# Experts in pairs: chunks of two experts alternate, and each down projection follows its chunk by one

## The chip, the cores and the metric

The kernel runs on one core of a Trainium2 chip. TensorE (PE) multiplies, PEld is its weight load, VectorE (DVE) and ScalarE (ACT) work on vectors, GpSimd (POOL) does little here, and SyncE (SP) issues the weight transfers. The metric is the device time of one execution in microseconds (us), the median of several runs.

## The reference

A backbone of two layers over 256 tokens of 1024 channels, batch 1, in float32. What matters here is the feed-forward part of the second layer, a SwiGLU of 8 experts with 3584 hidden channels, of which each token uses the two with the highest router logits:

```python
def moe_swiglu(h, w_router, b_router, w1, w3, w2):
    logits = (h @ w_router).astype(jnp.float32) + b_router.astype(jnp.float32)
    top_val, top_idx = lax.top_k(logits, TOP_K)
    top_w = jax.nn.softmax(top_val, axis=-1)
    gate = jnp.einsum('blk,blke->ble', top_w, jax.nn.one_hot(top_idx, N_EXPERTS, dtype=jnp.float32)).astype(h.dtype)
    out = jnp.zeros_like(h)
    for e in range(N_EXPERTS):
        out = out + gate[..., e:e + 1] * swiglu(h, w1[e], w3[e], w2[e])
    return out
```

With the given inputs the router sends 67, 37, 16, 137, 46, 15, 130 and 64 tokens to experts 0 to 7, 512 in all.

## The kernel before

Everything up to the router (both mixers, the dense feed-forward, the Fourier layer) is the same in both kernels. The experts' stage begins at about 579 us of the profiled execution.

**Positions.** Expert 0 comes first, since its weights can be loaded before the router is done. The others are sorted by their counts on the chip (L1345 to L1363), and `ORDER` (L29) says which rank stands at which position: 0, then ranks 6, 1, 7, 3, 2, 5, 4 (rank 1 has most tokens). Here the positions hold 67, 16, 137, 15, 64, 130, 37 and 46 tokens. The counts go into registers of PE, ACT and DVE (L1324, L1534), and the SP queue takes the experts' indices from registers (L1530).

**Units.** An expert's gathered tokens are handled in units of 64, at most three (`NU`, L1370); what lies past 192 tokens is left to a late pass (L1621 to L1642). A unit with 32 tokens or fewer in it runs as a half. Which units run is decided by nested `If`s on the counts, with an arm for the full and one for the half form: `base_unit` (L1417) for the first unit, `extra_units` (L1403) for the others, to the depth that `most` (L1391) bounds by the rank: the k-th largest count is at most 512 / k. So position 4 has code for three units and position 6 for two, whatever the counts. Position 0's first unit stands in no `If`.

**Chunks.** The 3584 hidden channels go in seven chunks of 512 (`NS`, L1368). For a chunk, `up_proj` (L1426) multiplies the unit's tokens with both up matrices in eight steps k, into one PSUM bank; SiLU on ACT (L1446) and the product on DVE (L1447) make the activations `a`. In the next chunk, at step k = 3, `flip` (L1449) transposes them, and DVE copies them to `aT` (L1454). `down_proj` (L1456) multiplies `aT` with the down matrix and adds into the expert's own PSUM bank over the seven chunks; after the last, `collect` (L1474) copies the sums to SBUF.

**Order.** The loop over positions (L1526) runs the up projection of expert e and the down projection of expert e - 1, chunk by chunk: up of the first unit in one `If`, up of the other units in a nest of `If`s, then the down projections in two more (for the first chunk the down projections come before the other units' up projections). All seven `aT` of the old expert are kept until then. After the eighth expert a ninth turn (`e == NE`) does seven chunks of down projections alone. Smaller work is put between the steps of the first unit's up projection (`work`, L1556): gate weights and scatter of the expert before the old one (L1557 to L1560, third unit L1608), one-hot and gather for the next expert (L1561 to L1565), the gate of the layer (L1567).

**Transfers.** All weights come through `load` (L60) on the SP queue, 1 MB each, into a ring of 18 slots. A chunk takes four for the up projection (`load_up`, L1513) and two for the down projection (`load_down`, L1518). A slot is free when the last arm that reads it has ended. The loads of the first expert are issued from 508 us on.

Of the kernel before, what the change touches and what calls it, by code (L numbers as in the profile page):

```python
# [11 lines left out]
OP = mybir.AluOpType  # L12
AX = mybir.AxisListType
# [15 lines left out]
ORDER = (0, 6, 1, 7, 3, 2, 5, 4)  # L29
# [5 lines left out]
def backbone(ctx, tc, x, c, cx, c_ctx, w_ada, b_ada, norm_g, w_in, short_w, short_b,  # L35
# [291 lines left out]
    # implicit filters and their spectra; even positions come first, then odd ones, and the second  # L327
    # half of the frequencies mirrors the first
# [142 lines left out]
    # the convolution branch, as a list of steps issued between the attention heads  # L471
# [247 lines left out]
    # the gate of a branch scales the columns of its last weights  # L719
# [6 lines left out]
    # the clock of the tensor engine falls while it idles  # L726
# [12 lines left out]
    # the same by column halves: the first half becomes the bias of the root  # L739
# [14 lines left out]
    # sums over the partitions: columns of two vectors at a time, or a row on all partitions  # L754
# [31 lines left out]
    with ExitStack() as es:  # L786
# [11 lines left out]
        # modulation vectors of what follows, a step of 256 rows of their weights at a time  # L798
# [70 lines left out]
        # the first one as its rows become ready  # L869
# [75 lines left out]
        for n in range(NU2):  # L945
# [44 lines left out]
            # the last ones wait, for the end  # L990
# [170 lines left out]
        # router weights for the raw rows  # L1161
# [76 lines left out]
    hg0 = [T(mp, [P, ND, P], f"hg0{b}") for b in range(2)]  # L1238
# [21 lines left out]
    with ExitStack() as es:  # L1260
        rp = mkpool("route", es=es)
        xT = T(rp, [P, 2, 2, 4, P], "xT")
        # logits from the raw rows, four parts of the channels side by side; scale and shift follow
# [35 lines left out]
        # places in the order of the logits, the first of equal ones before the others  # L1299
# [21 lines left out]
        nc.vector.tensor_copy(cnt[:, 2, 1:2], ps[0:1, 0:1])  # L1321
        gather(spread, P, hg0[0], [acc[1][0], acc[1][1]])
# [22 lines left out]
        # the experts after the first are taken in an order that follows their counts  # L1345
# [16 lines left out]
        nc.vector.reduce_max(key[0:1, 0:1], sorted_[0:1, 4, :], axis=AX.X)  # L1362
# [6 lines left out]
    NU = 3  # L1369
# [8 lines left out]
    ysb0 = T(up, [P, 2, 512], "ysb0")  # L1378
    ysb1 = T(up, [P, 512], "ysb1")
# [8 lines left out]
    LATE = 64 * NU  # L1388
    side = lambda u, j: j ^ (u & 1)
    # the k-th largest of the sorted counts is at most S * 2 / k  # L1390
    most = lambda e: S if e == 0 else min(S, 2 * S // ORDER[e])  # L1391

    class Expert:
        def __init__(self, e):
            self.e = e

        def rows(self, u):
            return hg1 if u == 2 else hg0[self.e % 2][:, :, 64 * u:64 * u + 64]

        def low(self, u, i):  # L1400
            return 64 * ((self.e * NS + i) % 2 if u == 0 else u % 2)

    def extra_units(E_, fn):  # L1403
        def level(u):
            with tc.If(counts[E_.e] > 64 * u):  # L1405
# [7 lines left out]
                if u < NU - 1 and most(E_.e) > 64 * (u + 1):  # L1413
                    level(u + 1)
        level(1)

    def base_unit(E_, fn):  # L1417
        if E_.e == 0:
            fn(False)
            return  # L1420
        with tc.If(counts[E_.e] > 32) as arm:
            fn(False)
        with arm.Else():
            fn(True)
# [298 lines left out]
```

## Time and profile before

| | us |
|---|---|
| three runs | 1638.01, 1643.89, 1647.61 |
| median | 1643.89 |
| profiled execution: its own time | not listed beside the runs; its span stands for it |
| profiled execution: span, first to last instruction | 1633.9 |
| of it PE busy | 1485.8 (91%) |
| DVE, ACT busy | 616.3, 319.0 |
| moved by DMA in all | 470 MB, mean 288 GB/s |

The profile puts each instruction under the line that issued it; a line in a helper stands for all its calls. An instruction of PE that multiplies shows as MATMUL with its weight load beside it (PEld); a float32 matmul of the program shows as two. "PEq L1405" is PE's sequencer at the `If` of that line: a branch, or a semaphore that keeps count for the arm that wasn't taken. "x" gives a number of instructions, brackets the idle time of the engine before it and what ended it.

### The profile page before, as it was taken

The page shows a single profiled execution, that of the slowest core. Times are in us where ns is not written, and L with a number is a line of the kernel's source. Part 1 is how long each engine was busy: PE and PEld are TensorE (multiplying, and loading weights), DVE is VectorE, ACT ScalarE, POOL GpSimd, SP SyncE. Part 2 cuts the span into 40 slices and gives each one's busy share as a digit, 9 for nine tenths or more (in the row PEclk, how much of TensorE's full clock was granted, in tenths as well). Part 3 has the DMA queues.
Part 4 walks back from the last instruction along what each step waited for, and adds up shares of the span by engine and source line. Part 5 has one row for each costly group of instructions (what it writes and reads, how often), then busy time and mean ns, then how long its engine had stood idle before and what let it go on. Part 6 is the DMA issues. An engine that isn't in the chain of part 4 may idle for free. (4 is left out here: it accounts for less than half of the span.)

```text
span 1633.9 us, 24684 instructions
## 1 busy us (share of the span) xinstructions
PE 1485.8 (91%) x9671; PEld 786.1 (48%) x9671; DVE 616.3 (38%) x933; ACT 319.0 (20%) x599; POOL 194.9 (12%) x139
## 2 busy tenths in 40 slices
PE   6999997899997889989999999867799999999886
PEld 1798685789996744333333334322333333333222
DVE  3547878699998721101111210220111111112222
ACT  2435443544444410000000000000000000000001
POOL 2412334333425300000000000000000000000000
PEclk9999897999999999999999999979899999999999
DMA  9336270599996758999997899998957777899991
GB/s 350 118 108 224 84 245 26 189 313 339 330 342 229 246 202 296 335 392 393 392 345 266 297 374 366 392 392 319 390 194 283 281 258 291 317 393 391 350 404 47
DMA packets 205484, 469.87 MB, mean 288 GB/s; under 512 B 8559, under 2 KB 43728, under 8 KB 204168
## 3 DMA queue, kind: packets, MB, share of 16 engines
q1 hardware_dynamic: 202576, 462.03, 77.1%
q8 instruction: 176, 2.88, 0.7%
q0 software_dynamic: 1680, 2.29, 0.7%
q10 hardware_dynamic: 1000, 2.24, 0.4%
q14 instruction: 52, 0.43, 0.1%
HBM read 465.48 MB, written 1.05 MB: 286 GB/s over the span
## 5 line engine op out<-in xcount | busy, mean ns | idle before, releaser
L1438 PE MATMUL w<-w,hg 128*64 128x512 f32 x1216 | 285.9, 604 | 20.8 <-PEq L1405 20.0
L1469 PE MATMUL y<-w,aT 128*64 128x512 f32 x896 | 214.6, 607 | 18.4 <-PEq L1405 10.3
L1454 DVE COPY aT<-w 128x256 f32<-128x256 f32 (+1 forms) x91 | 34.0, 373 | 401.2 <-PE w L1453 401.1
L1438 PEld LDWEIGHTS w<-w,hg 128*64 128x64 f32 x1216 | 86.8, 138 | 188.4 <-issue 183.5
L1438 PE MATMUL y<-w,hg 128*64 128x512 f32 x576 | 145.0, 607 | 8.0 <-PEq L1405 4.3
L1446 ACT ACTIVATE a<-w 64x512 f32<-64x512 f32 (+1 forms) x67 | 33.4, 498 | 599.0 <-PE w L1438 404.8
L1469 PEld LDWEIGHTS y<-w,aT 128*64 128x64 f32 x896 | 63.0, 138 | 152.4 <-issue 143.2
L1434 PE MATMUL w<-w,hg 128*32 128x256 f32 x1856 | 114.6, 389 | 9.7 <-PEq L1588 4.5
L1447 DVE TENSOR_TENSOR a<-a,w 64x512 f32<-64x512 f32 (+1 forms) x67 | 38.2, 570 | 211.4 <-ACT a L1446 155.6
L106 PE MATMUL f<-hh,wh 128*128 128x256 f32 x344 | 97.4, 283 | 0.7 <-ACT hh L937 0.7
L107 PE MATMUL f<-hl,wh 128*128 128x256 f32 x344 | 96.8, 281 | 0.5 <-POOL hl L938 0.4
L108 PE MATMUL f<-hh,wl 128*128 128x256 f32 x344 | 96.7, 281 | 0.0
L1434 PEld LDWEIGHTS w<-w,hg 128*32 128x32 f32 x1856 | 57.6, 111 | 66.7 <-issue 34.2
L1438 PEld LDWEIGHTS y<-w,hg 128*64 128x64 f32 x576 | 41.0, 138 | 84.8 <-issue 82.9
L114 POOL TENSOR_TENSOR wsl<-w,wsh 128x1024 fp32r<-128x1024 f32 x21 | 59.3, 2826 | 144.0 <-ACT wsh L113 144.0
L1462 PE MATMUL y<-w,aT 128*32 128x512 f32 x560 | 69.8, 618 | 6.6 <-PEq L1405 6.6
L113 ACT CAST wsh<-w 128x1024 fp32r<-128x1024 f32 x57 | 59.5, 1046 | 74.2 <-PE a L107 51.2
L114 DVE TENSOR_TENSOR wl<-w,wh 128x1024 fp32r<-128x1024 f32 x43 | 70.2, 1674 | 3.6 <-ACT wh L113 3.6
L106 PEld LDWEIGHTS f<-hh,wh 128*128 128x128 f32 x344 | 64.8, 188 | 2.0 <-ACT hh L937 1.0
L107 PEld LDWEIGHTS f<-hl,wh 128*128 128x128 f32 x344 | 64.8, 188 | 1.8 <-POOL hl L938 0.6
L108 PEld LDWEIGHTS f<-hh,wl 128*128 128x128 f32 x344 | 64.8, 188 | 0.0
L114 DVE TENSOR_TENSOR wsl<-w,wsh 128x1024 fp32r<-128x1024 f32 x36 | 47.2, 1313 | 37.7 <-ACT wsh L113 37.5
(455 smaller groups left out, 2134.7 us busy)
## 6 DMA issues: line engine op xcount, KB each, us to landing
w<-in_moe_w_dram SPq DMA_DIRECT2D x336, 1024.0 KB
w<-in_w_ada_dram SPq DMA_DIRECT2D x44, 1024.0 KB
w<-in_ffn_w_dram SPq DMA_DIRECT2D x33, 1024.0 KB
w<-in_w_in_dram SPq DMA_DIRECT2D x12, 1024.0 KB
w<-in_w_mix_out_dram SPq DMA_DIRECT2D x4, 1024.0 KB
w<-in_w_fourier_dram SPq DMA_DIRECT2D x4, 1024.0 KB
s<-in_w_ada_dram SPq DMA_DIRECT2D x2, 1024.0 KB
raw<-in_na_rpb_dram POOLq DMA_DIRECT2D x32, 62.5 KB, 2.7
```

Of the source, the lines that this page charges most:

```text
L106: nc.tensor.matmul(ps, lh, rh, start=first, stop=False)
L107: nc.tensor.matmul(ps, lh, rl, start=False, stop=False)
L108: last_mm[0] = nc.tensor.matmul(ps, ll, rh, start=False, stop=last).ins
L113: nc.scalar.copy(hi, src)
L114: (eng or nc.vector).tensor_sub(lo, src, hi.bitcast(F32))
L1434: ins = nc.tensor.matmul(ps[32 * j:32 * j + 32, 0:256], hg[:, k, 0:32], w, start=(k == 0), stop=(k == ND - 1), tile_position=(0, 32 * j)).ins
L1438: ins = nc.tensor.matmul(ps[64 * j:64 * j + 64, :], hg[:, k, 0:64], ws[j][k // 4][:, k % 4, :], start=(k == 0), stop=(k == ND - 1), tile_p ...
L1446: nc.scalar.activation(a[b3:b3 + 64, 0:n], ps[b1:b1 + 64, 0:n], AF.Silu)
L1447: nc.vector.tensor_mul(a[b3:b3 + 64, 0:n], a[b3:b3 + 64, 0:n], ps[b3:b3 + 64, 0:n])
L1454: nc.vector.tensor_copy(dst[:, 0:nb, :], tp[:, 0:nb, :])
L1462: nc.tensor.matmul(y[32 * j:32 * j + 32, :], aT[:, f, 32 * q:32 * q + 32], w2[fc // 2][:, fc % 2, h * 512:(h + 1) * 512], start=(i == 0 an ...
L1469: nc.tensor.matmul(y[64 * j:64 * j + 64, :], aT[:, f, :], w2[f // 2][:, f % 2, h * 512:(h + 1) * 512], start=(i == 0 and f == 0), stop=(i ...
```

## The change

Experts run in four pairs. Expert 0 and expert 1 are the first pair, both with weights that are known in advance; the other six are sorted, and `ORDER` pairs the largest with the smallest, the third with the fourth, the second with the fifth of them: 67 and 37, 137 and 15, 64 and 46, 130 and 16 tokens. The first of a pair (A) has up to three units, the second (B) up to two; the late pass takes what lies past 192 and 128 tokens. The chunks of A and B alternate. In one arm of one `If` a unit now does its up projection of chunk i and its down projection of chunk i - 1 (`step`), so `aT` is kept once per unit instead of seven times. The last down projection of a pair (`last_down`, with its transposes directly before it) follows in the first chunk of the next pair, and after the loop for the last pair. PSUM has three work banks instead of four and five for the sums of a pair; the first and third unit share a work bank. The activations of B have one buffer. The gather for expert 1 is put into the first chunk; the scatters of the old pair go into chunks 1 to 4, the gathers of the next one into chunks 5 and 6. In the diff comments are left out on the new side; lines outside of the experts' stage that lose only a comment aren't shown.

```diff
-ORDER = (0, 6, 1, 7, 3, 2, 5, 4)
+ORDER = (0, 1, 2, 7, 4, 5, 3, 6)
...
-    hg0 = [T(mp, [P, ND, P], f"hg0{b}") for b in range(2)]
+    hgs = [[T(mp, [P, ND, P], f"hg{k}{b}") for b in range(2)] for k in "ab"]
...
-        _, counts = nc.values_load_multi_w_load_instructions(cnt[0:1, 2, 1:2], engines=EN, min_val=0, max_val=S)
+        _, counts = nc.values_load_multi_w_load_instructions(cnt[0:1, 2, 1:3], engines=EN, min_val=0, max_val=S)
...
+        second = hgs[1][1].rearrange("p (t a) b -> p t (a b)", t=2)
+        one_hot(second, 1, rank, 0, P)
...
-    acts = [T(up, [P, 512], f"a{n}") for n in range(2)]
-    actT = [[T(up, [P, 4, 64], f"aT{u}_{j}") for j in range(NS)] for u in range(NU)]
...
-    ys_ps = [T(psYM, [P, 512], f"y{u}") for u in range(NU + 1)]
-    banks = [T(psW, [P, 512], f"w{b}") for b in range(4)]
-    fbank = banks[3]
+    UNITS = (3, 2)
+    acts = [T(up, [P, 512], f"a{n}") for n in range(3)]
+    actT = [[T(up, [P, 4, 64], f"aT{k}{u}") for u in range(UNITS[k])] for k in range(2)]
+    ys_ps = [[T(psYM, [P, 512], f"y{k}{u}") for u in range(UNITS[k])] for k in range(2)]
+    banks = [T(psW, [P, 512], f"w{b}") for b in range(3)]
+    fbank = banks[2]
...
-    most = lambda e: S if e == 0 else min(S, 2 * S // ORDER[e])
+    most = lambda e: S if e < 2 else min(S, 2 * S // (ORDER[e] - 1))
...
+    def do_up(E_, u, half, i, w, work=()):
+        at = {3: [lambda: flip(E_.act(u), E_.low(u, i - 1), half, E_.aT[u])]} if i else {}
+        for k, fn in work:
+            at.setdefault(k, []).append(fn)
+        up_proj(banks[u % 2], E_.rows(u), E_.act(u), E_.low(u, i), half, *w, at)
+
+    def do_down(E_, u, half, i, w2, gt=None):
+        if i == NS - 1:
+            flip(E_.act(u), E_.low(u, i), half, E_.aT[u])
+        down_proj(E_.ys[u], E_.aT[u], u, half, i, w2)
+        if i == NS - 1:
+            collect(E_.ys[u], u, half, (ysb1, ysb1) if u == 2 else (E_.ysb[:, 0, :], E_.ysb[:, 1, :]), gt)
+
+    def last_down(E_, w2, gt=None):
+        fn = lambda E_, u, half: do_down(E_, u, half, NS - 1, w2, gt)
+        base_unit(E_, fn)
+        extra_units(E_, fn)
...
-            if e < NE:
-                w1, w3 = load_up(e, i)
-                base_unit(cur, lambda half: do_up(cur, 0, half, work))
-            else:
-                for k, fn in work:
-                    fn()
-            if e > 0:
-                w2 = load_down(e - 1, i)
...
-            def all_down():
-                if e > 0:
-                    base_unit(old, lambda half: do_down(old, 0, half))
-                    extra_units(old, do_down)
-
-            # the last activations of the old expert leave their place before new ones take it
-            if first:
-                all_down()
-            if e < NE:
-                extra_units(cur, do_up)
...
-            if not first:
-                all_down()
+            def step(E_, u, half, w, w2, work=()):
+                do_up(E_, u, half, i, w, work)
+                if i:
+                    do_down(E_, u, half, i - 1, w2)
+
+            w = load_up(A.e, i)
+            w2 = load_down(A.e, i - 1) if i else load_down(old[0].e, NS - 1) if old else None
+            base_unit(A, lambda E_, u, half: step(E_, u, half, w, w2, work))
...
+            if old and first:
+                last_down(old[0], w2)
+            extra_units(A, lambda E_, u, half: step(E_, u, half, w, w2))
...
+            w = load_up(B.e, i)
+            w2 = load_down(B.e, i - 1) if i else load_down(old[1].e, NS - 1) if old else None
+            if old and first:
+                last_down(old[1], w2)
+            base_unit(B, lambda E_, u, half: step(E_, u, half, w, w2))
+            extra_units(B, lambda E_, u, half: step(E_, u, half, w, w2))
...
-        past, old, cur = old, cur, nxt
+        old, cur = cur, nxt
+    for E_ in old:
+        last_down(E_, load_down(E_.e, NS - 1), gt)
...
-    scatter(0, spread, ysb0, [banks[b] for b in (0, 2, 3, 1)])
+    free = [*banks, *ys_ps[0], *ys_ps[1]]
+    scatter(0, spread, old[0].ysb, free[:4])
+    scatter(0, tail_spread, old[1].ysb, free[4:])
```

## Rows read from the trace of the kernel before

**Rows 1.** Stretches, one per position and the tail: length, busy time, PEclk, DMA share, GB/s.

```profile
579.00:680.50 101.50, 92.71 (x741) 37.33 (x740) 20.16 (x62) 10.47 (x21) 0.00 (x0) 0.97 0.74 268
680.50:772.50 92.00, 81.00 (x753) 34.06 (x755) 10.48 (x27) 6.03 (x16) 0.00 (x0) 1.00 1.00 377
772.50:931.50 159.00, 155.83 (x1118) 58.18 (x1114) 27.34 (x58) 13.00 (x26) 0.00 (x0) 1.00 0.87 324
931.50:1043.30 111.80, 103.72 (x856) 41.29 (x852) 17.17 (x38) 4.73 (x12) 0.00 (x0) 0.98 1.01 375
1043.30:1172.10 128.80, 96.74 (x452) 35.61 (x448) 20.70 (x44) 7.89 (x17) 0.00 (x0) 0.87 0.98 369
1172.10:1343.00 170.90, 167.79 (x1117) 62.58 (x1116) 28.31 (x58) 13.00 (x26) 0.00 (x0) 1.00 0.71 261
1343.00:1473.30 130.30, 126.63 (x642) 42.68 (x640) 19.58 (x37) 6.23 (x12) 0.00 (x0) 1.00 0.90 336
1473.30:1575.00 101.70, 90.24 (x382) 28.79 (x378) 19.60 (x40) 6.84 (x12) 0.00 (x0) 0.97 1.00 378
1575.00:1634.00 59.00, 41.56 (x152) 13.43 (x152) 16.97 (x27) 4.65 (x8) 0.00 (x0) 0.91 0.40 155
```

**Rows 2.** Waits of PE, 579 to 1625 us: total us, times, longest.

```profile
PE w L1438 <- PEq L1405: 20.0, 22, 4.9
PE y L1469 <- PEq L1405: 10.3, 18, 1.5
...
PE y L1469 <- DMA w<-in_moe_w_dram: 3.3, 2, 2.9
...
PE y L1438 <- DMA w<-in_moe_w_dram: 1.1, 1, 1.1
```

**Rows 3.** PE's branches of L1405 at positions 2, 4, 6: ns min/median/max.

```profile
L1405 PEldq COMPARE_BRANCH  x21: 65/70/342, 780.6 to 929.2; - x21
...
L1405 PEldq COMPARE_BRANCH  x14: 208/832/7586, 1050.6 to 1168.5; - x14
...
L1405 PEldq COMPARE_BRANCH  x21: 65/65/3397, 1351.1 to 1467.3; - x21
```

**Rows 4.** Timeline of PE, position 4: start, us, instruction, idle before it.

```profile
1072.29 6.16 PE L1438 MATMUL w<-w,hg 128*64 128x512 f32 x16 [4.74 <-PEq L1405]
...
1118.85 5.07 PE L1438 MATMUL w<-w,hg 128*64 128x512 f32 x16 [4.88 <-PEq L1405]
...
1131.07 2.79 PE L1462 MATMUL y<-w,aT 128*32 128x512 f32 x16 [3.17 <-PEq L1405]
...
1147.27 1.92 PE L1462 MATMUL y<-w,aT 128*32 128x512 f32 x16 [3.40 <-PEq L1405]
...
1162.06 3.27 PE L1250 MATMUL w<-spread,x 128*128 128x64 f32 x17 [4.78 <-PEq L1405]
```

**Rows 5.** Timeline of PE, position 6, between up and down projection.

```profile
1429.96 7.09 PE L1469 MATMUL y<-w,aT 128*64 128x512 f32 x32 [0.33 <-PEq L1405]
```

**Rows 6.** Timeline of PE, position 1.

```profile
711.95 1.08 PE L1469 MATMUL y<-w,aT 128*64 128x512 f32 x4 [1.53 <-PEq L1405]
```

**Rows 7.** Timeline of PE, position 5: full up, half up, full down.

```profile
1210.31 3.65 PE L1438 MATMUL w<-w,hg 128*64 128x512 f32 x16 [0.45 <-PEq L1405]
...
1217.86 1.93 PE L1434 MATMUL w<-w,hg 128*32 128x256 f32 x32
...
1231.33 3.65 PE L1469 MATMUL y<-w,aT 128*64 128x512 f32 x16
```

**Rows 8.** Timeline of DVE and PEld around transposes at position 1.

```profile
686.03 0.42 DVE L1447 TENSOR_TENSOR a<-a,w 64x256 f32<-64x256 f32 x1 [4.23 <-ACT a L1446]
...
686.49 0.42 DVE L1454 COPY aT<-w 128x256 f32<-128x256 f32 x1
...
687.76 0.20 PEld L1453 LDWEIGHTS w<-ident,a 64*128 64x128 f32 x2 [0.81 <-DVE aT L1454]
```

**Rows 9.** The page, DMA queues: packets, MB, share of 16 engines.

```profile
q8 instruction: 176, 2.88, 0.7%
```

More of the change, by code (lines that the diff above doesn't have):

```diff
@@ L1412, in level @@
                     fn(E_, u, True)
-                if u < NU - 1 and most(E_.e) > 64 * (u + 1):
+                if u < UNITS[E_.k] - 1 and most(E_.e) > 64 * (u + 1):
                     level(u + 1)
@@ L1556, in backbone @@
-            work = []
-            if past is not None and i in (1, 2):
-                if i == 1:
-                    work.append((2, lambda: weights(past, 0, spread, banks[1])))
-                work.append((7, lambda: scatter(0, spread, ysb0, [banks[1], fbank], (i - 1,))))
-            if e < NE - 1 and i == 3:
-                nxt = Expert(e + 1)
-                one_hot(spread, nxt.e, sorted_, 0, 192)
-                work += [(5 + 2 * kh, lambda kh=kh: gather(spread, P, hg0[nxt.e % 2], [fbank, banks[1]], (kh,)))
-                         for kh in range(2)]
@@ L1567, in backbone @@
-            if e == NE - 1 and i == 3:
-                diag = hg0[NE % 2]
-                gt = diag.rearrange("p (h a) b -> p h (a b)", h=2)
+            work = []
+            if p == 0 and first:
+                work += [(2 + 3 * kh, lambda kh=kh: gather(second, P, B.hg, [fbank, banks[1]], (kh,))) for kh in range(2)]
+            if old and 1 <= i <= 4:
+                E_, t = old[(i - 1) // 2], (i - 1) % 2
+                if t == 0:
+                    work.append((2, lambda: weights(E_, 0, spread, banks[1])))
+                work.append((7, lambda: scatter(0, spread, E_.ysb, [banks[1], fbank], (t,))))
@@ L1570, in backbone @@
+            if nxt and i >= 5:
+                E_ = nxt[6 - i]
+                one_hot(spread, E_.e, sorted_, 0, P if E_.k else P + 64)
+                work += [(5 + 2 * kh, lambda kh=kh: gather(spread, P, E_.hg, [fbank, banks[1]], (kh,))) for kh in range(2)]
+            if not nxt and i == 5:
+                diag = hgs[0][NP % 2]
+                gt = wide(diag)
                 nc.vector.tensor_tensor(diag, ident.unsqueeze(1).to_broadcast([P, ND, P]),
@@ L1577, in backbone @@
                 work += [(5, lambda: gate_rows(0, fbank)), (7, lambda: gate_rows(1, banks[1]))]
-            if e < NE:
-                w1, w3 = load_up(e, i)
-                base_unit(cur, lambda half: do_up(cur, 0, half, work))
-            else:
-                for k, fn in work:
-                    fn()
-            if e > 0:
-                w2 = load_down(e - 1, i)
-            if e == 0 and first:
+            if not nxt and last:
+                work += [(4, lambda: weights(A, 0, spread, banks[1])), (6, lambda: weights(B, 0, tail_spread, banks[1]))]
@@ L1596, in backbone @@
-            if first:
-                all_down()
-            if e < NE:
-                extra_units(cur, do_up)
-            if e == 0 and i == 1:
+            if old and first:
+                last_down(old[0], w2)
+            extra_units(A, lambda E_, u, half: step(E_, u, half, w, w2))
+            if old and i == 2 and most(old[0].e) > P:
+                with tc.If(counts[old[0].e] > P):
+                    weights(old[0], 2, spread, banks[1])
+                    scatter(2, spread, ysb1, [fbank, banks[1]])
@@ L1605, in backbone @@
-            if last and nxt is not None and most(nxt.e) > P:
-                with tc.If(counts[nxt.e] > P):
+            if nxt and last and most(nxt[0].e) > P:
+                with tc.If(counts[nxt[0].e] > P):
                     gather(spread[:, :, P:], 64, hg1, banks[1:3])
-            if past is not None and i == 2 and most(past.e) > P:
-                with tc.If(counts[past.e] > P):
-                    weights(past, 2, spread, banks[1])
-                    scatter(2, spread, ysb1, [fbank, banks[1]])
@@ L1643, in backbone @@
-    scatter(0, spread, ysb0, [banks[b] for b in (0, 2, 3, 1)])
-    if most(past.e) > P:
-        with tc.If(counts[past.e] > P):
-            weights(past, 2, spread, banks[1])
-            scatter(2, spread, ysb1, [banks[b] for b in (0, 2, 3, 1)])
+            for s0 in range(64 * UNITS[e % 2], min(S, most(e)), 64):
+                with tc.If(late[e] > s0):
+                    E_ = Expert(e)
+                    sp = hg1.rearrange("p (t a) b -> p t (a b)", t=2)
+                    hg = hgs[0][1 - NP % 2]
+                    one_hot(sp, e, sorted_, s0, 64)
+                    gather(sp, 64, hg, banks[1:3])
+                    for i in range(NS):
+                        w1, w3 = load_up(e, i)
+                        w2 = load_down(e, i)
+                        up_proj(banks[0], hg, acts[0], 64, False, w1, w3, {})
+                        flip(acts[0], 64, False, actT[0][0])
+                        down_proj(ys_ps[0][0], actT[0][0], 0, False, i, w2)
+                    collect(ys_ps[0][0], 0, False, (acts[1], acts[1]), gt)
+                    weights(E_, s0 // 64, sp, banks[1])
+                    scatter(s0 // 64, sp, acts[1], [fbank, banks[1]])
@@ L1649, in backbone @@
+    free = [*banks, *ys_ps[0], *ys_ps[1]]
+    scatter(0, spread, old[0].ysb, free[:4])
+    scatter(0, tail_spread, old[1].ysb, free[4:])
+    if most(old[0].e) > P:
+        with tc.If(counts[old[0].e] > P):
+            weights(old[0], 2, spread, banks[1])
+            scatter(2, spread, ysb1, free[2:6])
     with ExitStack() as es:
```

94 lines of the change are left out of this document (37 added, 57 removed).

## The prediction

> **What bounds the kernel now.** The times of the runs are 1638.01, 1643.89 and 1647.61 us; a difference of 0.5%, 8.2 us, is about what a measurement of this kernel can tell from no change. The profiled execution has a span of 1633.9 us, and some 10 us lie around a span if the median is taken for it. All sums below are differences, so I add them to 1643.9.
>
> First I read the experts' stage in stretches, one for each position of the order, from the first up projection of one to that of the next [rows 1]. Stretch length less PE busy is PE's idle time: 8.8 us at position 0, then 11.0, 3.2, 8.1, 32.1, 3.1, 3.7, 11.5, and 17.4 in the tail. The reader is to see two things. PE is busy for 956 of 1055 us, so the stage is bound by PE; and DMA is now full (0.98 to 1.01 of its time at positions 1, 3, 4, 7), now at 0.71 (position 5). This is the unevenness that the change evens out. So the second view asks whether PE ever waits for the weights: of its waits, those for weight DMAs come to 3.3 and 1.1 us in the two largest rows [rows 2]. Those for PEq, its own sequencer, are 20.0 and 10.3 us in two rows alone. **Evening out the transfers is worth some 5 us at most, and I take zero**, for where a branch and a weight load end together the row cannot part them.
>
> The third view tells what PEq is: the branches of the Ifs [rows 3]. At position 2 the longest takes 0.34 us. At position 4 the median is 0.83 and the longest 7.59 us. At position 6 the longest is 3.40 us. The timeline shows what PE feels of them. At position 4 it stands still for 4.74, 4.88, 3.17, 3.40 and 4.78 us, mean 4.2, each time behind PEq [rows 4]. At position 6, between up and down projection (where the 3.17 and 3.40 stood), it stands still for 0.33 us only [rows 5], since matmuls were still queued while the branch took its time.
>
> What differs is how much program is jumped over. A full up projection shows 16 + 16 matmuls around its transposes (the first 16 in [rows 7]), each matmul with a weight load of its own (the two counts of rows 1 run alike), so 64 instructions; a half one 32 + 32 matmuls [rows 7], 128; a down projection 16 matmuls [rows 4, 7], 32. With transposes (four or two, doubled) an arm of the up If is 72 or 132 instructions. Position 6 holds one full unit and may hold two: it jumps its half arm and one untaken level, 132 + 72 + 132 = 336. Position 4 may hold three units: 132 + 2 x 204 = 540. So 336 instructions cost 0.33 us, 540 cost 4.2. The instruction queue moves 176 packets and 2.88 MB, 16.4 KB each [rows 9]: I read it so that the program comes from memory in blocks, and that a far jump has to wait for one.
>
> **What the change does, part by part.**
>
> *Work of PE: zero.* The router's counts (67, 37, 16, 137, 46, 15, 130, 64 by expert) fill the same units of 64 and halves of 32 as before, and every unit keeps its matmuls. Gathers, weights and scatters are the same in number. No expert reaches the late pass (A's pass 192, B's 128).
>
> *Idle time that goes.* At 2 and 5 there is one gap of about 0.45 us per chunk [rows 7], 3.15 us per position; it stands behind an If that isn't taken, where PE first runs dry. What positions 1, 3 and 4 have above that is 7.9, 4.9 and 28.9 us. These far jumps disappear in their present form: **-41.7 us**. Position 0's start, position 7 and the tail I leave as they are.
>
> *Fewer gaps at untaken Ifs.* Up and down now share an arm, so a pair of chunks has four groups of Ifs where two chunks of the old order have eight. Eight positions at 3.15 us are 25.2. Afterwards pairs 0, 1 and 3 have one plain gap per pair chunk (E0's third level, E5, E2), 9.45 us; the others are priced next. **-15.75 us.**
>
> *Longer jumps.* A fused arm is 72 + 32 = 104 instructions full, 132 + 32 = 164 half. E7 (64 tokens, third pair; may have three units by the bound) jumps 164 + 2 x 268 = 700. That is past the 540 of position 4, so I take its 4.2 us, seven chunks: **+29.4**; bounds 0.33 (all hidden) and 4.88 (the longest of rows 4) give 2 and 34. E1 (37 tokens) and E4 (46) jump 164 + 268 = 432, halfway between 336 and 540: bounds 0.33 and 4.2 us for 14 chunks, 5 to 59. I take 1.4, nearer the hidden end, because the fused arm ends in a down projection that leaves as much work queued as position 6's up projection does, and position 1's jumps show 1.53 us [rows 6]: **+19.6**. E2 and E0's third level jump 268, less than 336: the plain gap already counted.
>
> *The last transposes.* Each of 13 units ends with its transposes directly before its down projection, where the old order had an up projection in between. PE then waits for DVE's copy; the nearest row has 0.81 us for such a wait [rows 8], bounds 0.4 (the copy alone is 0.42) and 1.0: **+10.4**, 5 to 13.
>
> *Transposes within a chunk: zero.* They stand at the fourth of eight steps as before, and the four steps that follow take 1.9 us or more [rows 7], against a copy of 0.42 [rows 8]. If that cover were gone, it would be 0.8 us a unit.
>
> *Fewer PSUM banks: zero.* The first unit always uses one bank now, so the next expert's first unit waits until SiLU and product have read it. A down projection stands between, 1.92 us at the least [rows 4], and the product after the SiLU takes 0.42 [rows 8]. Behind it is all of B, so if it fails, 0.5 us for each of 14 half units is 7 us.
>
> *SP's queue.* Six loads instead of four and two go out at each release. The ring has 18 slots and PE holds six, so twelve are ahead; at 378 GB/s [rows 1] a load of 1.05 MB takes 2.77 us. The third pair has 84 loads, 233 us, 33 of them ahead: 200. Its two full units take 11.1 us each per chunk (7.55 from the start of one unit's up projection to the next, 3.6 down [rows 7]), 155 us for seven pair chunks, and with 39 us of jumps and some 35 of gathers, scatters and the second pair's last down projections PE needs 230. Transfers stay hidden: zero.
>
> *The end.* The seven pure down projections shrink to one for each of two experts, but these are PE's work either way. Two experts and a third unit scatter after the last If: +2 us, bounds -5 and +8.
>
> *Clock.* Position 4 runs at 0.87 [rows 1], behind its idle gaps; a stage with the same gaps (the third pair) pays the same: zero.
>
> Sum: -41.7 - 15.75 + 29.4 + 19.6 + 10.4 + 2 = **+4 us, so 1648 us**. The stalls change places.
>
> **The rivals.**
>
> *Faster: far jumps stay hidden.* Place: the branch behind a fused arm in E1, E4 and E7. It decides whether the branch takes less than the matmuls still queued, about 3 us going by position 6 (a 3.40 us branch [rows 3], 0.33 us gaps [rows 5]). Then 21 jumps cost 0.33 us, 6.9 instead of 49: 1648 - 42 = **1606**. For it: position 6 had DMA at 0.90 and still hid them, and the release of slots is more regular. Against: position 4 with 7.59.
>
> *Slower: all of the 432s stall like the 540s.* Then E1 and E4 cost 14 x 4.2 = 59 instead of 20: 1648 + 39 = **1687**. For it: two jumps in succession, with no matmul between, as at position 4. Against: 432 is nearer to 336.
>
> [...]
>
> *Bound by transfers in the third pair.* If its lead were gone at the start, 84 loads take 233 us and the last unit's 11 come after: 14 us over my 230, **1662**. Against: the second pair chunk has three full units' worth of work (two full, two half) and its own gathers, over 34 us for 33 us of loads, so the ring is full when the third pair begins.
>
> **How the numbers follow.** Forecast 0.42 (its own range 1635 to 1664, by the bounds of E1, E4 and of the transposes), faster rival 0.28, slower rival 0.25, transfers 0.05. Faster by over 0.5% (under 1636): the rival and the forecast's low edge, 0.31. Within 0.5%: 0.26, nearly all from the forecast. Slower (over 1652): 0.43. The range reaches to both rivals: 1606 to 1690.
>
> **What would show it.** The branches' longest and median by pair: about 3 us in pairs 0 and 2, E7's with gaps near 4 us, and under 0.5 us in the second pair. PE's waits for PEq total about what they were, but in other places; waits for weight DMAs stay under 10 us. DMA's share is even, 0.85 to 1.0 in all pairs. Thirteen PE waits of 0.8 us for DVE's aT. If PE idles for weights in the third pair, or PEq's waits fall under 30 us, or rise over 100, the forecast is wrong.

## The result, and the profile after

The kernel after takes 1686.01 us (median of four runs, 1683.0 to 1691.16), the kernel before 1645.22 (four runs, 1638.01 to 1647.61). The ratio is **1.0272, 95% interval 1.0231 to 1.0313: slower by 41 us**. The profiled execution of after took 1683.0 us, with a span of 1681.2; before's span is 1633.9.

From 579 us on, the stage takes 1102.2 us instead of 1055.0. PE is busy for 964.8 of them instead of 956.2, with as many matmuls (6204 records against 6191). So of the 47.2 us in the spans 38.6 are idle time, and 8.6 are the same work at a lower clock (granted 0.94 on average, 0.97 before). The stretches of the kernel after, one for each pair and the tail, with the columns of [rows 1] (length; busy time of PE, PEld, DVE, ACT, POOL; PEclk, DMA share, GB/s):

```profile
579.00:825.36 246.36, 218.41 (x1391) 91.15 (x1389) 32.46 (x92) 20.90 (x45) 1.84 (x2) 0.95 0.89 332
825.36:1087.85 262.49, 253.85 (x1944) 99.06 (x1943) 42.10 (x91) 17.79 (x38) 0.00 (x0) 0.99 0.85 315
1087.85:1348.22 260.37, 208.28 (x894) 75.34 (x895) 40.34 (x79) 14.16 (x29) 0.00 (x0) 0.89 0.97 360
1348.22:1628.10 279.88, 256.01 (x1878) 94.25 (x1877) 43.41 (x94) 17.12 (x34) 0.00 (x0) 0.96 0.76 284
1628.10:1681.20 53.10, 28.25 (x102) 9.53 (x102) 21.53 (x36) 4.43 (x8) 0.00 (x0) 0.76 0.09 31
```

PE idles for 28.0 us in the first pair, 8.6 in the second, **52.1 in the third**, 23.9 in the fourth and 24.9 in the tail. The second pair, whose units nearly all run, is nearly as good as the best positions of before, 2, 5 and 6 in [rows 1]. PE's waits, from 575 us on (engine and line, what for, us in total, times, longest):

```profile
PE w L1447 <- PEq L1414: 41.7, 22, 4.9
PE w L1447 <- DMA w<-in_moe_w_dram: 21.7, 6, 5.4
PE y L1478 <- DVE aT L1463: 9.1, 7, 1.6
PE y L1478 <- PEq L1414: 9.1, 6, 3.6
PE y L1471 <- DVE aT L1463: 5.3, 5, 1.6
PE w L1462 <- issue: 4.8, 1, 4.8
```

Taken at its word, the second row would be waits for weights, 21.7 us where before had 3.3 and 1.1 [rows 2]. It isn't so. PE's branches of L1414, the `If`s of the extra units, in the second pair, in the third, and then the one in the third pair that begins at 1249.4 us:

```profile
L1414 PEldq COMPARE_BRANCH  x25: 73/78/3167, 830.8 to 1084.7; - x25
...
L1414 PEldq COMPARE_BRANCH  x17: 73/5820/7642, 1097.0 to 1336.6; - x17
...
L1414 PEldq COMPARE_BRANCH  x1: 7642/7642/7642, 1249.4 to 1249.4; - x1
```

The last one ends at 1257.0. The timeline of PE in the third pair shows what waited for it:

```profile
1147.82 6.48 PE L1447 MATMUL w<-w,hgb 128*64 128x512 f32 x16 [4.70 <-PEq L1414]
...
1163.90 5.27 PE L1447 MATMUL w<-w,hga 128*64 128x512 f32 x16 [2.20 <-DMA w<-in_moe_w_dram]
...
1257.54 6.23 PE L1447 MATMUL w<-w,hgb 128*64 128x512 f32 x16 [4.83 <-DMA w<-in_moe_w_dram]
```

The gap put down to a DMA ends half a microsecond behind the 7.64 us branch, and it is as long as expert 7's gaps that stand under PEq (4.67 to 4.91). The 2.20 at 1163.90 likewise ends behind a branch of 5.82 us that began at 1157.6. So do all six of the row: each ends some 0.5 us behind a branch of 5.8 to 7.6 us, just as the 4.70 at 1147.82 does, which stands under PEq. The branch is therefore taken for what ended them, though the profile names the load; the run with short arms below bears this out. Six gaps of 4.67 to 4.91 us stand behind expert 7's first unit, and gaps of 2.18 to 2.27 behind four of expert 4's.

In such a gap the transfers run dry too, since a slot comes free only when an arm ends (from 579 us on SP's queue waits for PEq L1414 41 times, 298.3 us in all). The DMA queues between 1143.1 and 1147.8 us (packets, MB, share of the 16 engines): the weights fill 58.8% of the time, and the instruction queue moves two packets:

```profile
q1 hardware_dynamic: 284, 1.07, 58.8%
q8 instruction: 2, 0.03, 4.8%
```

Counted branch by branch, the instruction queue (q8) tells the long branches from the short ones. Of the 17 branches of the third pair, the six of expert 7 that take 7.44 to 7.64 us hold two of its packets each, five of expert 4's, 3.51 to 5.88 us, hold one each, and the six under 0.6 us none.

### The profile page after: what moved, and what is told of

It is laid out like the page before. It is cut to its first block, busy times and chain, and to the rows that moved or that the text cites. A ratio compares the mean times of both kernels' runs of the same rounds, so it can differ in the third digit from the quotient of the medians.

```text
span 1681.2 us, 24098 instructions
## 1 busy us (share of the span) xinstructions
PE 1492.6 (89%) x9671; PEld 800.0 (48%) x9671; DVE 616.4 (37%) x935; ACT 319.3 (19%) x599; POOL 196.3 (12%) x140
## 5 line engine op out<-in xcount | busy, mean ns | idle before, releaser
L1447 PE MATMUL w<-w,hga 128*64 128x512 f32 x1344 | 336.5, 628 | 46.3 <-PEq L1414 26.2
L1447 PEld LDWEIGHTS w<-w,hga 128*64 128x64 f32 x1344 | 100.3, 143 | 230.4 <-issue 226.1
L1455 ACT ACTIVATE a<-w 64x512 f32<-64x512 f32 (+1 forms) x91 | 46.4, 510 | 796.5 <-PE w L1447 576.6
L1456 DVE TENSOR_TENSOR a<-a,w 64x512 f32<-64x512 f32 (+1 forms) x91 | 52.9, 582 | 300.9 <-ACT a L1455 179.5
L1447 PE MATMUL w<-w,hgb 128*64 128x512 f32 x448 | 119.7, 663 | 26.1 <-PEq L1414 15.4
L1447 PEld LDWEIGHTS w<-w,hgb 128*64 128x64 f32 x448 | 38.9, 153 | 94.5 <-issue 91.0
L114 DVE TENSOR_TENSOR wsl<-w,wsh 128x1024 fp32r<-128x1024 f32 x36 | 47.2, 1313 | 37.9 <-ACT wsh L113 37.9
L1462 PEld LDWEIGHTS w<-ident,a 64*128 64x128 f32 x294 | 25.2, 139 | 69.6 <-issue 65.8
L106 PE MATMUL a<-hxh,wsh 128*128 128x256 f32 x192 | 55.2, 288 | 1.0 <-DVE z L476 1.0
```

Source lines behind the costliest of these rows:

```text
L106: nc.tensor.matmul(ps, lh, rh, start=first, stop=False)
L114: (eng or nc.vector).tensor_sub(lo, src, hi.bitcast(F32))
L1447: ins = nc.tensor.matmul(ps[64 * j:64 * j + 64, :], hg[:, k, 0:64], ws[j][k // 4][:, k % 4, :], start=(k == 0), stop=(k == ND - 1), tile_p ...
L1455: nc.scalar.activation(a[b3:b3 + 64, 0:n], ps[b1:b1 + 64, 0:n], AF.Silu)
L1456: nc.vector.tensor_mul(a[b3:b3 + 64, 0:n], a[b3:b3 + 64, 0:n], ps[b3:b3 + 64, 0:n])
L1462: nc.tensor.transpose(tp[:, b, :], a[b3:b3 + 64, b * P:(b + 1) * P], ident[b3:b3 + 64, b3:b3 + 64])
```

## The experiments

Theory J: PE stalls by the program that branches jump over, and the fused arms made those jumps longer. Its rivals: the transfers bind the third pair (T); the branches and semaphores cost, not the length (S); the transposes ahead of the last down projections. The kernel before was run again beside each group, at 1639.7 to 1643.0 us, so kernels of different groups are compared by their ratios to it; 0.01 is 16.4 us.

### The unrun code made short, in both kernels

In units that these counts never run, an arm keeps its `If`s but holds little:

```diff
+    def stub(E_, u, w):
+        nc.tensor.matmul(banks[u % 2][0:64, :], E_.rows(u)[:, 0, 0:64], w[:, 0, 0:512], start=True, stop=True, tile_position=(0, 0))
+        a = E_.act(u)[64 * (u % 2):64 * (u % 2) + 64, :]
+        nc.scalar.activation(a, banks[u % 2][0:64, :], AF.Silu)
+        nc.vector.tensor_mul(a, a, a)
...
+        def fn(E_, u, half):
+            if RUN[E_.e] > 64 * u:
+                real(E_, u, half)
+            else:
+                stub(E_, u, w)
```

> The kernel after, with every If and every arm kept, but in units that these counts never run (expert 0's third, expert 1's second, expert 7's second and third, expert 4's and expert 2's second) the arm holds one matmul, one SiLU and one product instead of its 64 to 128 matmuls. These arms are not taken, so nothing that runs is changed. Theory J (what costs is the length of the program that a branch jumps over): the third pair's idle of 52.1 us falls to about 12, the first pair's 28.0 to about 14, the fourth's 23.9 to about 12, and the 8.6 us by which PE was busier at a lower clock come back: 1686 - 75 = about 1611 if the transfers keep up. Theory J with transfers as the next bound (T): the third pair's 84 loads at 2.7 us are 227 to 233 us, so it cannot fall from 260 to 212 us but to about 233, with PE then waiting for weight DMAs: about 1632. Rival S (the branches and semaphores themselves cost, whatever stands between them): within 0.5% of 1686.

Measured: 1596.43 us, ratio 0.9726 (0.9705 to 0.9748): **90 us below after, though every instruction that ran is the same**. The five stretches:

```profile
579.00:799.99 220.99, 209.59 (x1400) 87.15 (x1399) 32.46 (x92) 21.12 (x45) 1.84 (x2) 0.99 0.93 350
799.99:1065.18 265.19, 255.35 (x1944) 98.92 (x1943) 41.92 (x91) 17.79 (x38) 0.00 (x0) 0.99 0.88 330
1065.18:1277.53 212.35, 191.77 (x895) 70.28 (x895) 39.04 (x78) 14.15 (x29) 0.00 (x0) 0.97 1.04 393
1277.53:1539.74 262.21, 250.55 (x1877) 92.59 (x1876) 44.45 (x95) 17.12 (x34) 0.00 (x0) 0.99 0.90 339
1539.74:1594.30 54.56, 27.95 (x106) 9.42 (x102) 21.54 (x36) 4.43 (x8) 0.00 (x0) 0.73 0.08 30
```

S is out. T is out for the kernel after: the third pair took 212 us, less than the 227 to 233 that T held for its floor, since the loads that were ahead at its start count too (82.88 MB moved in it, 79 loads, not 84). Its waits and branches (first the wait for weights, then the branches of L1428, which is L1414 of after):

```profile
PE w L1461 <- DMA w<-in_moe_w_dram: 5.6, 4, 2.7
...
L1428 PEldq COMPARE_BRANCH  x17: 65/218/347, 1074.3 to 1261.4; - x17
```

The same 17 branches have a median of 0.22 us instead of 5.82. In the whole pair the instruction queue moves 19 packets, where it moves 40 in after's third pair. The saving was larger than the 75 expected, and it is the clock's share that was larger: PE is busy for 935.2 us instead of 964.8, 29.6 us less for the same work at a granted clock of 0.97 instead of 0.94, beside some 57 us less idle.

> The kernel before with its Ifs and arms kept and one matmul, SiLU and product in the arms of units that these counts never run: the twin of the kernel after with short arms (1596). It parts what the Ifs cost from what the length of the jumps costs. By theory J an If of such a unit costs the same in both kernels: 1596 - 1572 = 24 us for after's 48 (six experts, seven chunks and a last down projection each); before has 84 (six positions, seven chunks, up and down apart), 42 us: 1556 + 42 = about 1598. The long jumps are then 1642 - 1598 = 44 us of before and 1686 - 1596 = 90 of after. If it stands at 1560 to 1570, the Ifs themselves cost before nothing and its long jumps 75 or more, and the change lost only some 15 us by them.

Measured: 1586.44 us, 0.9678 (0.9659 to 0.9697), between the two numbers that were named. The long jumps cost before 0.0322, 53 us, and after 1.0272 - 0.9726 = 0.0546, 90 us. **The change adds 37 us of them** (by the intervals some 8 us more or less); that is most of its loss.

### The unrun code taken out, with its Ifs

```diff
+    RUN = (67, 37, 137, 15, 64, 46, 130, 16)
...
-                if u < UNITS[E_.k] - 1 and most(E_.e) > 64 * (u + 1):
+                if u < UNITS[E_.k] - 1 and most(E_.e) > 64 * (u + 1) and RUN[E_.e] > 64 * (u + 1):
                     level(u + 1)
-        level(1)
+        if RUN[E_.e] > 64:
+            level(1)
```

> The kernel after, without any code for the units that these counts never run (their Ifs are gone too). Theory J: as with the short arms, and up to 0.45 us less for each If that is gone, about 36 of them where PE had run dry: 1595 to 1611 if transfers keep up; J with T: about 1630, the third pair at 228 to 235 us. Rival S: part of the stalls goes with the branches here, but not in the run with short arms. If the waits of the third pair that the profile puts down to weight DMAs (16.3 us) were really for DMAs, they stay or grow here.

> The kernel before, without any code for the units that these counts never run: the same edit. Theory J alone: the 41.7 us that positions 1, 3 and 4 idle above a plain position go, most of position 7's 11.5, part of the 0.45 us gaps, and some 8 us of low clock: 1645 - 55 = about 1590, below after's twin. J with T: a position has 42 loads, 42 x 2.67 = 112 us at full rate; position 4 cannot fall from 129 below 112, and positions 1 and 3 already move at 1.00 of the DMAs' time, so at most some 17 us go there and PE starts to wait for weights: about 1620 to 1630. If both twins stand at the same time, or after's stands lower, the even transfers of the change are worth something that the jumps hid; if before's stands lower by 20 us or more, they are worth nothing.

Measured: after without that code 1572.28 us, 0.9580 (0.9559 to 0.9601); before without it 1556.33, 0.9474 (0.9451 to 0.9497). Both are below what J gave, since without the `If`s themselves more goes than it had allowed: 0.9726 - 0.9580 = 0.0146 in after, 24 us, and 0.9678 - 0.9474 = 0.0204 in before, 33 us. PE's waits for weights stay at 9.8 us in after's version and 9.3 + 3.5 in before's: in before, too, the uneven transfers that seemed to bind positions 1, 3 and 4 bind little once the jumps are gone.

### One step of the length, and a shift

```diff
-                if u < UNITS[E_.k] - 1 and most(E_.e) > 64 * (u + 1):
+                if u < UNITS[E_.k] - 1 and most(E_.e) > 64 * (u + 1) and (E_.e, u) != (4, 1):
```

> The kernel after, with the code of one unit left out that these counts never run: expert 7's third. The branch behind its first unit then jumps 164 + 268 = 432 instructions instead of 700, as expert 4's does. Theory J with the price by length: expert 7's gaps fall from 4.8 to the 2.1 us of expert 4's, 7 x 2.7 = 19 less, and a little clock: about 1665. Rival (any far jump costs the same, and the 4.8 us come from something else of expert 7, such as the weights that the profile names): within 0.5% of 1686.

Measured: 1663.32 us, 1.0148 (1.0095 to 1.0201), 20 us below after by the ratios, as expected. Behind expert 7 and expert 4 (PE's timeline), and the branches of both:

```profile
1150.38 5.35 PE L1447 MATMUL w<-w,hgb 128*64 128x512 f32 x16 [3.02 <-PEq L1414]
...
1165.49 3.65 PE L1447 MATMUL w<-w,hga 128*64 128x512 f32 x16 [2.35 <-PEq L1414]
...
L1414 PEldq COMPARE_BRANCH  x18: 65/5812/6134, 1089.4 to 1324.0; - x18
```

With 432 instead of 700 instructions the longest branch falls from 7.64 to 6.13 us, and the six gaps of 4.67 to 4.91 become five of 2.98 to 3.46 and one of 0.44: shorter, as J says, but five of them not as short as expert 4's. Between 1143.0 us and 1150.3, where the gap of 3.02 ends, the instruction queue moves one packet; after's branch of 7.44 us holds two.

The shift:

```diff
+    with tc.If(counts[0] > 255):
+        for _ in range(32):
+            nc.tensor.matmul(banks[1][:, 0:P], ident, ident, start=True, stop=True)
     for p in range(NP):
```

> The kernel after, with 32 matmuls in an If ahead of the experts' loop that isn't taken: all code behind it moves by some 128 instructions of PE, and nothing else changes. If a stall goes by where the target lies in blocks of program, the uneven gaps change: those of expert 2 (0.65 to 5.4 us by chunk) and of expert 0's third unit (0.3 to 3.6 us) move to other chunks or other sizes, and the total moves by up to 15 us either way. If a stall goes by the length of the jump alone, every gap stays as it was, within 0.3 us, and the total at 1686 plus at most 4 for the new If.

Measured: 1684.12 us, 1.0256 (1.0201 to 1.0311); the new `If` shows a gap of 11.2 us, where 4 at most had been expected. That gap is no price of a jump: its branch takes 0.37 us and begins only at 590.1. In the kernel after, the stage's first `If` (L1604) has its branch at 588.7, and PE works meanwhile on matmuls that stand ahead of it; what the sequencer waits for until then isn't shown. PE's idle time from 575 us on rises from 137.6 to 142.2 us, so the other gaps together shrank by 6.5. What is to be seen is expert 2's gaps, ahead of chunks 1 to 4 of expert 6 in the kernel after:

```profile
1386.41 5.39 PE L1447 MATMUL w<-w,hga 128*64 128x512 f32 x12 [4.23 <-PEq L1414]
...
1427.54 3.65 PE L1447 MATMUL w<-w,hga 128*64 128x512 f32 x16 [1.09 <-PEq L1414]
...
1470.98 4.47 PE L1447 MATMUL w<-w,hga 128*64 128x512 f32 x12 [5.40 <-DMA w<-in_moe_w_dram]
...
1510.44 3.65 PE L1447 MATMUL w<-w,hga 128*64 128x512 f32 x16 [0.65 <-PEq L1414]
```

and ahead of the same four chunks with the shift:

```profile
1393.84 2.79 PE L1447 MATMUL w<-w,hga 128*64 128x512 f32 x12 [1.21 <-DVEq L1414]
...
1435.03 6.04 PE L1447 MATMUL w<-w,hga 128*64 128x512 f32 x16 [4.05 <-DMA w<-in_moe_w_dram]
...
1474.86 2.79 PE L1447 MATMUL w<-w,hga 128*64 128x512 f32 x12 [1.36 <-PEq L1414]
...
1517.37 5.83 PE L1447 MATMUL w<-w,hga 128*64 128x512 f32 x16 [5.37 <-PEq L1414]
```

Over the six chunks after has 4.23, 1.09, 5.40, 0.65, 4.69 and 2.15 us, the shifted kernel 1.21, 4.05, 1.36, 5.37, 2.01 and 0.46: long and short have changed places. A jump of 268 instructions stalls or not by **where it lies**; of the jumps of expert 7, 700 long, six stay at 4.71 to 5.30 us, and the one in the first chunk falls from 4.83 to 3.61. Since every edit here moves the code behind it, a difference of a few us between kernels that have long jumps can come from that alone (an estimate from the 6.5 us here).

### Up and down in arms of their own again

```diff
-            base_unit(A, lambda E_, u, half: step(E_, u, half, w, w2, work))
+            base_unit(A, ups(w, work))
...
-            extra_units(A, lambda E_, u, half: step(E_, u, half, w, w2))
+            extra_units(A, ups(w))
+            if i:
+                base_unit(A, downs(w2))
+                extra_units(A, downs(w2))
```

The same is done for B.

> The kernel after, with pairs and the one-chunk lag kept, but up and down projection of a unit in arms and Ifs of their own again: half arms of 132 and 32 instructions instead of one of 164. The branches of the up projections then jump 540 (expert 7), 336 (experts 1 and 4) and 204 (expert 0's third, expert 2's second). Theory J: expert 7's gaps stay near 4.2, those of 1 and 4 fall from 2.1 to 0.4 (-20 us), expert 0's and 2's to 0.45 (-15), and 0.45 us of gap comes back for about three more Ifs per pair chunk (24 x 1.3 = +32): 1675 to 1690. If the fused arm itself is most of the loss: under 1660. If it is a gain by the Ifs that it saves, with the jumps no shorter: over 1700.

Measured: 1712.50 us, 1.0447 (1.0401 to 1.0494), above the whole range that J had been given, where the third case, a gain by the `If`s that are saved, had been put. The jumps are shorter and more: PE's waits for PEq and for what the profile calls issue, which here stands ahead of down projections:

```profile
PE w L1447 <- PEq L1414: 30.7, 28, 6.5
PE y L1478 <- PEq L1414: 21.9, 17, 4.6
PE y L1471 <- issue: 19.3, 5, 5.0
```

So the expectation fell, and with it the thought that the fused arm is the loss: it saves more at `If`s than its length adds, 0.0175 or 29 us. Nor is there much more code to jump over. By the prediction's counts (a unit's level is 268 instructions, half alone 164) the levels that never run are 1668 instructions in a chunk of every position of before and 1772 in after. What is left is the order: expert 1's jumps, hidden at position 6 beside down projections of the 130-token expert [rows 5], now follow work of its own pair, and two experts with nothing but jumps behind one unit stand side by side in the third pair. Another pairing was not tried, so this stays an argument; nor is it parted how much of the 37 us is the order and how much the places where the jumps happen to lie.

### The last transposes

```diff
     def do_down(E_, u, half, i, w2, gt=None):
-        if i == NS - 1:
-            flip(E_.act(u), E_.low(u, i), half, E_.aT[u])
         down_proj(E_.ys[u], E_.aT[u], u, half, i, w2)
...
                 if i:
                     do_down(E_, u, half, i - 1, w2)
+                if last:
+                    flip(E_.act(u), E_.low(u, i), half, E_.aT[u])
```

> The kernel after, with the last transposes of a unit at the end of its arm in the last chunk (behind the down projection there) instead of directly before the last down projection. By the trace PE waits for DVE's aT twelve times at 0.4 to 1.6 us, 14.4 us in all, seven of them within full arms. If these waits are worth their length: 1686 - 13 = 1673. If they only cover another wait (the branch behind, the low clock at the end): within 0.5% of 1686.

Measured: 1670.31 us, 1.0185 (1.0154 to 1.0215): 14 us by the ratios. The waits were longer than the row of before had shown; DVE's timeline says why (kernel after, last down projections of the second pair):

```profile
1100.37 1.39 DVE L1491 COPY ysb<-y 64x512 f32<-64x512 f32 x2 [3.76 <-PE y L1478]
1101.79 0.42 DVE L1463 COPY aT<-w 128x256 f32<-128x256 f32 x1
```

The copy of `aT`, 0.42 us, stands on DVE behind the copies of the sums of the unit before, 1.39 us, which the down projection has just released. In the order of before these were never beside each other.

> The kernel after, without code for the units that never run (1572) and with the last transposes at the end of the arm of the last chunk. The twin of before without that code stands at 1556. If the waits for the last transposes (15.4 us in that run, plus 1.6 twice for the third unit's sum) are what is left of the change's loss: 1556 to 1560, equal to before's twin within 0.5%; then pairing, even transfers and fewer Ifs are worth nothing beside each other. If the low clock or the tail holds it: 1565 or more. If even transfers are worth something: below 1550.

> The kernel after with short arms in the units that never run (1596) and with the last transposes at the end of the last arm: the change without its two losses, to be held against before's twin with short arms (1586). The transposes were worth 16 us in after and 14 without the unrun code: 1596 - 15 = 1581, some 5 us below before's twin, by the Ifs that pairs save (48 of unrun units instead of 84). If transfers bind the third pair instead, as the 18.4 us of waits for weight DMAs in the version without that code suggest, PE waits for them there and it stands at 1585 to 1592: then the change has nothing to give here even without its losses.

Measured: 1557.95 us, 0.9492 (0.9458 to 0.9526), against 0.9474 for before's twin, the same within the intervals; and 1578.97 us, 0.9613 (0.9595 to 0.9630), against 0.9678 (0.9659 to 0.9697) for the twin with short arms. With neither long jumps nor late transposes **the change saves 0.0065, some 11 us, and nothing where there are no such `If`s**. This fits its fewer `If`s, which by the pairs of runs above cost 24 us and not 33. The even transfers give nothing that these runs can show: without the unrun code and the late transposes PE waits 18.4 us for weights in the paired order.

So the change's 0.0272 is made of three parts: the longer jumps, 0.0546 - 0.0322 = +0.0224 (37 us); the transposes, with short arms, 0.9726 - 0.9613 = +0.0113 (19 us); the fewer `If`s, 0.9613 - 0.9678 = -0.0065 (-11 us). They add up by the way they are formed; what bears on them from outside is the 14 us of the transposes in the kernel after itself, and the 33 - 24 = 9 us of the `If`s.

### A version that beats both, and the same rule on the kernel after

The kernel before, with the units that have code set by rank, and the rest left to the late pass (whose code takes any unit now; that part is left out here). With these counts the late pass runs nothing, so its own time wasn't measured.

```diff
+    LIM = [3 if e == 0 or ORDER[e] < 3 else 2 if ORDER[e] < 6 else 1 for e in range(NE)]
...
-                if u < NU - 1 and most(E_.e) > 64 * (u + 1):
+                if u < LIM[E_.e] - 1 and most(E_.e) > 64 * (u + 1):
                     level(u + 1)
-        level(1)
+        if LIM[E_.e] > 1:
+            level(1)
```

> A version meant to beat both, for any counts: the kernel before, with the number of units that have code set by rank (three for expert 0 and ranks 1 and 2, two for ranks 3 to 5, one for ranks 6 and 7), and what lies past them left to the late pass, which runs none of it here. Position 4 then jumps 336 instructions instead of 540, positions 1 and 3 only their half arm of 132. Theory J: position 4's idle falls from 32.1 to position 6's 3.7, positions 1 and 3 to 3 to 5, and some 5 us of clock come back: 1642 - 28 - 12 - 5 = about 1597. Rival (position 4 idles because its light predecessor leaves transfers at 0.98 of their time): not below 1625.

Measured: **1602.51 us, 0.9771 (0.9736 to 0.9805)**: 38 us below before and 82 below after. Position 4, of 128.8 us before, takes:

```profile
1024.74:1134.91 110.17, 92.71 (x452) 34.71 (x448) 20.70 (x44) 7.91 (x17) 0.00 (x0) 0.91 1.04 393
```

So it was not held at 128.8 by transfers, as the rival had it; at a DMA share of 1.04 they may hold it now. PE still idles there for 17.5 us, where 3.7 had been expected: jumps of 336 instructions and less cost 2.74 to 3.13 us in four places; the branches there take 1.30 to 5.92 us, with a median of 5.03 (six, 1047 to 1118 us). Two of the four gaps:

```profile
1083.50 5.33 PE L1443 MATMUL w<-w,hg 128*64 128x512 f32 x16 [2.74 <-PEq L1409]
...
1110.19 3.08 PE L1467 MATMUL y<-w,aT 128*32 128x512 f32 x16 [3.13 <-PEq L1409]
```

> The kernel after for any counts, with the rule of the version that beats both (units that have code set by rank: three for expert 0 and the two largest, one for the two smallest, two for the rest) and the last transposes at the end of the last arm. Theory J: 16 us for the transposes, 23 for expert 7's third unit, and most of the 18 us of expert 2's gaps above a plain one: about 1629, still above the 1602 of before with that rule, since experts 1, 4 and 7 go on jumping 432. Rival (pairing pays once the worst jumps are gone): at or below 1602.

Measured: 1621.37 us, 0.9894 (0.9874 to 0.9914), 8 us below the expectation, below before and above the version on before, as expected.

## Why the prediction was right and wrong

It said slower as the likeliest of the three, with 1648 as its number; it is 38 us more, outside the forecast's own 1635 to 1664 and inside the wide range that reaches to both rivals. The number of the slower rival, 1687, is almost the result, but not by that rival's mechanism: experts 1 and 4 did not stall like the 540s. So that the result lies in the range, which its upper edge owes to that rival, is in part luck.

| step | predicted, us | measured |
|---|---|---|
| PE's work, SP's queue, PSUM banks | 0 | 0: as many matmuls; waits for weights 5.6 us in the third pair once the jumps are short |
| positions 1, 3, 4 above a plain gap | -41.7 | these positions are gone; not measured apart |
| plain gaps at Ifs | -15.75 | gaps up to 0.6 us that end with PEq: 47 with 19.5 us before, 12 with 5.5 after, -14.1 |
| expert 7, jump of 700 | +29.4 | six gaps of 4.67 to 4.91 and one of 4.83 in the first chunk, 33.4 |
| experts 1 and 4, jump of 432 | +19.6 | 14 gaps, 0.31 to 4.01, together 26.9 |
| experts 0 and 2, jump of 268 | 0 beyond a plain gap | 29.4 in 14 gaps, 23.1 beyond plain ones of 0.45 |
| last transposes | +10.4 | twelve waits, 14.4; taken away, 14 |
| clock | 0 | +8.6 of PE's busy time |
| end | +2 | tail's idle 17.4 to 24.9, 6.7 of it waits behind transposes and sums (5.1 of them are in the row of the transposes too) |

**Right:** that the stage is bound by PE and its branches and not by the weights; that the far jumps change places, from positions 1, 3 and 4 to experts 7, 4 and 1; the prices of 700 and, nearly, of 432; that evening out the transfers is worth about nothing.

**The step that failed** is the sentence that experts 2 and 0 "jump 268, less than 336: the plain gap already counted". It took the length as a threshold: 336 hidden at position 6, so 268 is too. The shift and the version on before show that there is none. Jumps of at most 336 cost 2.7 to 3.1 us at position 4 of the version on before, and the same 268 cost 0.65 or 5.40 us in neighbouring chunks, by where they lie in the program. Expert 2 alone has 18.6 us of gaps. The trace of before spoke against a threshold already. By the prediction's counts no jump at position 1 is longer than the 132 of a half arm, and it shows 1.53 us [rows 6]. And position 6 did not hide a stall at each of its jumps: of its seven branches over the unit that isn't run four take 0.21 to 0.22 us and one 1.17; only two take the 3.4 that [rows 3] gives as the longest. What the stalls go with is the place, as the shift shows (4.23 and 1.09 us become 1.21 and 4.05), and in the third pair the packets of the instruction queue: two in each branch of 7.44 to 7.64 us, none in those under 0.6.

**The second miss is the clock.** It was put at zero, since "a stage with the same gaps (the third pair) pays the same". There are more gaps, and the work behind the long ones is slower too. In the kernel after the 16 matmuls of L1447 behind a gap of 4.0 to 4.9 us take 5.07 to 6.58 us in seven places; behind gaps of 2.0 to 2.3 us they take 5.27 to 5.35 in three and 3.65 in five. The stretch of the gap at 1143, the 16 matmuls behind it, and the next 16 (columns as above, the third from the end is the granted clock):

```profile
1143.12:1147.82 4.70, 0.00 (x1) 0.03 (x1) 0.00 (x0) 0.00 (x0) 0.00 (x0) 0.88 0.63 232
1147.82:1154.30 6.48, 6.48 (x17) 1.96 (x18) 0.00 (x0) 0.00 (x0) 0.00 (x0) 0.56 0.91 316
1154.61:1158.26 3.65, 3.65 (x20) 1.35 (x20) 0.42 (x1) 0.00 (x0) 0.00 (x0) 1.00 1.05 388
```

The 16 matmuls take 6.48 us at a granted clock of 0.56, and the next 16 take 3.65 at 1.00: the gap of 4.70 costs 7.53.

**The transposes** were mis-sized by the row they were taken from, 0.81 us, with a free DVE: behind a finished unit DVE first has 1.39 us of copies, so a full unit waits up to 1.62; the twelve waits have a mean of 1.2.

Of the signs that had been named, PE's waits for PEq stayed between 30 and 100 us and moved; the DMA share, 0.76 to 0.97, was less even than said; and the third pair's idling for weights, which would have spoken against the forecast, was for the most part a label: 16.3 us in the kernel after, 5.6 with short arms.

## What to carry to other kernels

Code in an arm that never runs is not free: PE pays for jumping over it, in the kernel after by up to 5.4 us a jump and up to 2.9 more of slow matmuls behind it (6.58 us for 16 that take 3.65 elsewhere), so count the instructions between a taken arm and the next one, and give each level of such a nest code only where the data can often need it. A stall that seems hidden at one place is hidden by what is queued there (PE is busy through the branches of 3.37 and 3.40 us at position 6 of before, and its gaps are 0.33 and 0.40) and by where the jump lies (268 instructions show 0.65 or 5.40 us); it is no price for another place. To test it, empty the arms that aren't taken: nothing that runs changes, and the difference in time is the price.

## What the runs showed that was not expected

- Unrun code cost after 90 us and before 53, 5.5% and 3.2% of the time, without one instruction of it run.
- A shift of the program by some 128 instructions makes long and short stalls change places chunk by chunk (4.23 and 1.09 us become 1.21 and 4.05).
- In the third pair of the kernel after a branch's length goes with the packets of the instruction queue inside it: none under 0.6 us, one at 3.5 to 5.9, two at 7.4 to 7.6.
- An idle wait that the profile puts down to a weight DMA (21.7 us in six) can be a branch that ended some 0.5 us ahead of it; only the branch's own row, 5.8 to 7.6 us long and ended just ahead, tells.
- Of the 90 us, 29.6 are PE's busy time: the same matmuls at a granted clock of 0.94 instead of 0.97.
